# A matmul with LoRA, bound by DMA: fifteen partitions' second rows move from the software queue to a small store

## Chip, cores, metric

One core of a Trainium2 chip. The metric is the device time of one execution in microseconds (us); lower is better. The span in a profile is the time from the first to the last instruction and is about 1.3 us shorter than the time.

## The reference

```python
# x: 16 x 2048 x 256, W: 256 x 256, lora_A: 256 x 16, lora_B: 16 x 256, lora_E: 16; all float32
x_flat = x.reshape(-1, in_dim)                       # 32768 rows of 1024 bytes
y = x_flat @ W
lora_out = ((x_flat @ lora_A) * lora_E) @ lora_B
y = y + scale * lora_out
```

33.6 MB come in and 33.6 MB go out. The kernel folds the LoRA product into one 256 x 256 weight and then does one matmul, so bytes decide.

## The kernel before

The 32768 rows are four chunks of 128 partitions x 64 rows. A partition's 64 rows are one contiguous run of 64 KB in HBM. The ring in SBUF has three homes; a chunk is loaded, cast, turned, multiplied, and the result is written back to the home and stored from there. The order of loads (L) and stores (S) on the sync queue is a list:

```python
ORDER = [
    # ... cut: loads of chunks 0 to 3, stores of chunk 0
    ("S", 1, 0, 64),
    ("S", 2, 2, 62),      # chunk 2: rows 2 to 61 of each partition
    ("S", 3, 0, 64),
]
SHARED = 2
END_ROWS = 2
SHARES = (slice(108, 113), slice(0, 108), slice(113, P))
```

Chunk 2 is the shared one. Its rows 0, 1, 62 and 63 aren't in the large store; GpSimd's software queue writes them, in three shares of 5, 108 and 15 partitions:

```python
    def sync_program():
        # ... cut
            else:
                sync.wait_ge(s_done, -(-(c * ROWS + e) // CG) + NY)
                sync.dma_start(out=y_chunks[c, :, s:e, :], in_=at_home).then_inc(stored.get(op, stored_rest), 16)
        sync.wait_ge(shared_stored, 16 * len(SHARES))

    def share(engine, p, landed):
        def ends_of(at):
            return at[p].rearrange("p (q b) k -> p q b k", b=END_ROWS)[:, :: ROWS // END_ROWS - 1, :, :]

        engine.dma_start(out=ends_of(y_chunks[SHARED]), in_=ends_of(rows(SHARED, 0, ROWS))).then_inc(landed, 16)

    def gpsimd_program():
        # ... cut: the casts
        gpsimd.wait_ge(s_done, (SHARED + 1) * ROWS // CG + NY)
        for p in SHARES:
            share(gpsimd, p, shared_stored)
```

A large hardware store goes evenly to the 16 DMA engines, 8 partitions each. The software shares do not: they are there to give some engines less. The wait for the shares stands ahead of the closing barriers, the wait for the large stores behind them.

## Time and profile before

| | before |
|---|---|
| time, median of the first 3 runs / of 6 | 161.19 / 161.13 us |
| span of the profiled execution (its time: 161.41) | 160.1 us |
| bytes moved, mean rate | 67.41 MB, 421 GB/s |
| PE busy, ACT busy | 60%, 41% |
| last store issued, landed | 122.8, 160.0 us |

The DMA engines are busy from start to end, and compute is over at 122.7 us. The prediction below shows the lines.

In what follows, "large piece" is one hardware packet of 61440 or 65536 bytes (one partition of chunk 2 or 3), and "software packet" one packet of the shares (4096 bytes: one partition, two rows at either end). The trace has a start, a duration, a size and a queue for each packet and no engine number. The engines can be told apart nevertheless: on one engine a packet nearly always starts 3 to 4 ns before the end of the one before it, and each engine must have 8 pieces of each large store. I followed all 16 through the tail in this way; tables from it are in plain fences. A "heavy" engine is one of the twelve that carry ten software packets, a "light" one is one of the four that carry two.

### The profile page before, as it was taken

Reading aid. Unit: us, or ns where it says so; the run is one execution under the profiler, and the core shown is the slowest. Engines: PE = TensorE matmul, PEld = TensorE weight load, DVE = VectorE, ACT = ScalarE, POOL = GpSimd, SP = SyncE. Lnnn points to the kernel's source line nnn. Section 1 sums busy time; section 2 is a strip of 40 time slices with the busy share of each in tenths; the row PEclk is TensorE's granted clock in tenths of the full one; section 3 lists DMA queues with packets and bytes.
Section 4 is the critical chain, followed back from the end, with each engine's and each line's share of the span. In section 5 each row is a group of like instructions: output and inputs, shape, how many; then the busy total and the mean of one; then the engine's idle time right before and its main releaser. Section 6 shows DMA issues by size and latency. Waiting matters only on the chain.

```text
span 160.1 us, 2042 instructions
## 1 busy us (share of the span) xinstructions
PE 95.3 (60%) x782; PEld 83.3 (52%) x782; DVE 46.1 (29%) x67; ACT 66.3 (41%) x66; POOL 63.3 (40%) x41
## 2 busy tenths in 40 slices
PE   2749999999999910000799999999993000000000
PEld 1235899999999900000699999999992000000000
DVE  0113355555555510000155555555551000000000
ACT  3000577777777730000077777777775000000000
POOL 1044676777767100003676768686850000000000
PEclk9999999999999985555599999999999555555555
DMA  7999999999979997989999999996997998999965
GB/s 270 426 442 436 411 446 434 475 401 401 598 311 524 442 344 328 481 348 442 430 461 393 475 434 401 524 491 295 524 462 308 481 484 354 480 432 390 523 295 248
DMA packets 2449, 67.41 MB, mean 421 GB/s; under 512 B 512, under 2 KB 528, under 8 KB 784
## 3 DMA queue, kind: packets, MB, share of 16 engines
q1 hardware_dynamic: 2016, 66.60, 97.2%
q0 software_dynamic: 224, 0.52, 0.9%
q10 hardware_dynamic: 208, 0.28, 0.5%
q14 instruction: 1, 0.01, 0.0%
HBM read 33.85 MB, written 33.55 MB: 421 GB/s over the span
## 4 chain that ended last, share of the span: by engine, by line
PE 41%; DMA 32%; POOL 2%; ACT 1%; issue 0%; SPq 0%; ACTq 0%; POOLq 0%
DMA out_dram<-ring 27%; PE psum_y L271 26%; PE psum_xt L251 14%; DMA ring<-in_x_dram 5%; POOL stage L194 2%; PE psum_y L297 1%; ACT ring L217 1%; SPq L146 0%; ACTq L217 0%; POOLq L193 0%
## 5 line engine op out<-in xcount | busy, mean ns | idle before, releaser
L217 ACT COPY ring<-psum_y 128x1024 f32 x64 | 64.8, 1013 | 54.3 <-PE psum_y L271 54.3
L194 POOL CAST stage<-ring 128x2048 bf16<-128x2048 f32 x32 | 60.6, 1896 | 52.8 <-DMA out_dram<-ring 22.1
L271 PE MATMUL psum_y<-weff,xt 128*128 128x256 bf16 x512 | 68.5, 278 | 0.0
L240 DVE COPY xt<-psum_xt 128x1024 bf16<-128x1024 bf16 x64 | 44.3, 691 | 62.9 <-PE psum_xt L251 62.9
L251 PE MATMUL psum_xt<-ident,stage 128*128 128x128 f32 x260 | 41.3, 283 | 23.4 <-POOL stage L194 23.4
L271 PEld LDWEIGHTS psum_y<-weff,xt 128*128 128x128 bf16 x512 | 51.3, 100 | 6.0
L251 PEld LDWEIGHTS psum_xt<-ident,stage 128*128 128x128 f32 x260 | 31.6, 146 | 26.3 <-issue 25.2
L283 PE MATMUL psum_y<-ident 128*128 128x512 f32 x4 | 3.8, 1101 | 2.9 <-POOL ident L172 2.9
L283 PEld LDWEIGHTS psum_y<-ident 128*128 128x128 f32 x4 | 1.2, 324 | 3.9 <-POOL ident L172 2.9
L167 POOL DMA_DIRECT2D out_dram<-ring x3 | 2.0, 675 | 1.5 <-PE psum_y L271 1.5
L222 DVE TENSOR_SCALAR stage<-psum_y,e_sb 16x256 f32<-16x256 f32 x1 | 0.5, 472 | 7.2 <-PE psum_y L289 7.2
L211 ACT ACT_TABLE_LOAD x1 | 1.3, 1283 | 2.1 <-SPq L312 2.1
L297 PE MATMUL psum_y<-stage 16*128 16x256 f32 x4 | 2.1, 670 | 0.0
L231 DVE COPY xt<-psum_xt 128x1024 bf16<-128x1024 bf16 x1 | 0.7, 692 | 3.8 <-PE psum_xt L251 3.8
L297 PEld LDWEIGHTS psum_y<-stage 16*128 16x128 f32 x4 | 1.2, 319 | 0.5 <-issue 0.3
L234 DVE TENSOR_TENSOR weff<-stage,psum_y 128x512 bf16<-128x512 f32 x1 | 0.7, 686 | 1.4 <-PE psum_y L297 1.4
L289 PEld LDWEIGHTS psum_y<-ident,a_sb 128*16 128x16 f32 x2 | 0.3, 137 | 1.2 <-issue 1.2
L170 POOL MEMSET ident<- 128x128 f32 x1 | 0.2, 205 | 1.7 <-SPq L312 1.7
L289 PE MATMUL psum_y<-ident,a_sb 128*16 128x128 f32 x2 | 0.6, 421 | 0.0
L172 POOL TENSOR_SCALAR_AFFINE_SELECT ident<-ident 128x128 f32<-128x128 f32 x1 | 0.3, 283 | 0.2 <-POOL ident L170 0.2
L211 ACT COPY one<-ident 128x1 f32<-128x1 f32 x1 | 0.2, 191 | 0.0
L334 POOL MEMSET const-float32-0.0<- 128x1 f32 x1 | 0.1, 93 | 0.2 <-issue 0.2
(3 smaller groups left out, 0.3 us busy)
## 6 DMA issues: line engine op xcount, KB each, us to landing
ring<-in_x_dram SPq DMA_DIRECT2D x4, 4096.0 KB, 24.6
out_dram<-ring SPq DMA_DIRECT2D x1, 7680.0 KB, 37.1
ring<-in_x_dram SPq DMA_DIRECT2D x2, 3072.0 KB, 17.0
out_dram<-ring SPq DMA_DIRECT2D x1, 5120.0 KB, 43.0
out_dram<-ring SPq DMA_DIRECT2D x1, 3072.0 KB, 42.7
ring<-in_x_dram SPq DMA_DIRECT2D x1, 2048.0 KB, 7.9
out_dram<-ring POOLq DMA_DIRECT2D x1, 432.0 KB, 31.3
stage<-in_W_dram ACTq DMA_DIRECT2D x1, 256.0 KB, 2.8
```

What stands on the lines that cost most here:

```text
L167: engine.dma_start(out=ends_of(y_chunks[SHARED]), in_=ends_of(rows(SHARED, 0, ROWS))).then_inc(landed, 16)
L194: gpsimd.tensor_copy(out=stage[n % NS][:], in_=rows(c, b, b + CAST)).then_inc(s_stage[n % NS], 1)
L211: scalar.copy(out=one[:], in_=ident[:, :1])
L217: scalar.copy(out=to, in_=psum_y[i % NY][:]).then_inc(s_free[(i + NY) % UNROLL], 1)
L231: vector.tensor_copy(out=xt[0][:], in_=psum_xt[0][:].bitcast(BF16)).then_inc(s_xt[0], 1)
L234: vector.tensor_add(out=weff[:], in0=w_sb, in1=psum_y[1][:, :KT, :]).then_inc(s_free[0], 1)
L240: vector.tensor_copy(out=xt[g % NX][:], in_=psum_xt[g % NT][:].bitcast(BF16)).then_inc(s_xt[g % UNROLL], 1)
L251: ins = tensor.transpose(psum_xt[i % NT][:, b, :], words[:, at * CG + b, :], ident[:])
L271: ins = tensor.matmul(psum_y[i % NY][:, b, :], xt[i % NX][:, b, t::KT], weff[:, t, :], start=(t == 0), stop=(t == KT - 1),)
L283: ins = tensor.matmul(psum_y[1][:, :2, :], ident[:], ident[:, None, :].to_broadcast([P, 4, P]), start=True, stop=True)
L289: ins = tensor.transpose(psum_y[0][:R, t, :P], a_sb[:, t, :], ident[:])
L297: ins = tensor.matmul(psum_y[1][:, t, :], ate[:, t, :], b_sb, start=True, stop=True)
```

## The change

The last 15 partitions give the software queue only rows 0 and 63. Their rows 1 and 62 are written by a small store of 15 x 2 x 1024 bytes on the sync queue, between the large stores of chunks 2 and 3. By its form, the intent seems to be to take a little load from one DMA engine, since a store of 15 partitions uses 15 engines. Compute is unchanged.

```diff
-END_ROWS = 2
-SHARES = (slice(108, 113), slice(0, 108), slice(113, P))
+LAST = slice(113, P)
+SHARES = ((slice(108, 113), 2), (slice(0, 108), 2), (LAST, 1))
...
-    n_rest = sum(op[0] == "S" and op not in waited for op in ORDER)
+    n_rest = 1 + sum(op[0] == "S" and op not in waited for op in ORDER)
...
-                sync.wait_ge(s_done, -(-(c * ROWS + e) // CG) + NY)
+                sync.wait_ge(s_done, (c * ROWS + (ROWS if c == SHARED else e)) // CG + NY)
                 sync.dma_start(out=y_chunks[c, :, s:e, :], in_=at_home).then_inc(stored.get(op, stored_rest), 16)
+                if c == SHARED:
+                    second = slice(1, ROWS - 1, ROWS - 3)
+                    to, of = y_chunks[c, LAST, second, :], rows(c, 0, ROWS)[LAST, second, :]
+                    sync.dma_start(out=to, in_=of).then_inc(stored_rest, 16)
...
-        for p in SHARES:
-            share(gpsimd, p, shared_stored)
+        for p, n in SHARES:
+            share(gpsimd, p, n, shared_stored)      # n rows at either end
```

More of the change, by code (lines that the diff above doesn't have):

```diff
@@ L158, in sync_program, with share @@
             else:
-                sync.wait_ge(s_done, -(-(c * ROWS + e) // CG) + NY)
+                sync.wait_ge(s_done, (c * ROWS + (ROWS if c == SHARED else e)) // CG + NY)
                 sync.dma_start(out=y_chunks[c, :, s:e, :], in_=at_home).then_inc(stored.get(op, stored_rest), 16)
+                if c == SHARED:
+                    second = slice(1, ROWS - 1, ROWS - 3)
+                    to, of = y_chunks[c, LAST, second, :], rows(c, 0, ROWS)[LAST, second, :]
+                    sync.dma_start(out=to, in_=of).then_inc(stored_rest, 16)
         sync.wait_ge(shared_stored, 16 * len(SHARES))
-    def share(engine, p, landed):
+    def share(engine, p, n, landed):
         def ends_of(at):
-            return at[p].rearrange("p (q b) k -> p q b k", b=END_ROWS)[:, :: ROWS // END_ROWS - 1, :, :]
+            return at[p].rearrange("p (q b) k -> p q b k", b=n)[:, :: ROWS // n - 1, :, :]
         engine.dma_start(out=ends_of(y_chunks[SHARED]), in_=ends_of(rows(SHARED, 0, ROWS))).then_inc(landed, 16)
```

## The prediction

> **What bounds the kernel now.** I read the page of the profile first, then the chain of waits, the waits of the store queue, and the DMA view in narrow windows.
>
> ```profile
> PE   2749999999999910000799999999993000000000
> DMA  7999999999979997989999999996997998999965
> DMA packets 2449, 67.41 MB, mean 421 GB/s; under 512 B 512, under 2 KB 528, under 8 KB 784
> q1 hardware_dynamic: 2016, 66.60, 97.2%
> q0 software_dynamic: 224, 0.52, 0.9%
> HBM read 33.85 MB, written 33.55 MB: 421 GB/s over the span
> ```
>
> The matrix engine rests in about half of the slices; the DMA engines rest in none. 67.41 MB have to move whatever the order is, and the windows view gives 434 to 441 GB/s in the stretches without a gap (8 to 32 us, 74 to 150 us). 67.41 MB at 436 GB/s are 154.6 us of the 160.1 us span. What remains, 5.5 us, is the start, one lull near 58 us (loads to stores) and the tail. Compute is over long before the end: the answers of the timeline and of the store queue's waits are
>
> ```profile
> 121.70 1.01 ACT L217 COPY ring<-psum_y 128x1024 f32 x1 [0.30 <-PE psum_y L271]
> 122.83 0.33 SPq L160 DMA_DIRECT2D out_dram<-ring  x1
> ```
>
> ```profile
> SPq L160 <- PE psum_y L271: 54.6, 3, 27.1
> SPq L160 <- PEq L305: 19.4, 1, 19.4
> SPq L308 <- SPq L308: 3.8, 1, 3.8
> ```
>
> The last store is issued at 122.83 and lands 37.2 us later: the last 37 us are a queue being emptied. The last of the three lines says how far the two kinds of store differ at the end. The wait for the software queue's three shares ends near 155 us; after the closing barriers the core still sits 3.8 us in the wait for the big stores. So a share that lands up to 3.8 us later costs nothing.
>
> The end is therefore the last of 16 DMA engines, and the question is which one and why. The trace does not number them, but the DMA view in a narrow window counts a packet where it starts, so single engines can be seen. From 119.4 to 121.4 us (40 slices of 50 ns), where the first 61440-byte piece of chunk 2 starts on each engine, one piece is 1229 GB/s:
>
> ```profile
> DMA  0099999099099090000000000900000900000000
> GB/s 0 0 1229 1229 2458 2458 1229 0 1229 1229 0 3687 1229 0 1229 0 0 0 0 0 0 0 0 0 0 1229 0 0 0 0 0 1229 0 0 0 0 0 0 0 0
> ```
>
> 14 engines start it between 119.50 and 120.15, one at 120.65 and one at 120.95: two engines are late. From 156.1 to 160.1 us (slices of 100 ns), where each engine starts its last 65536-byte piece, one piece is 655 GB/s:
>
> ```profile
> DMA  9909999000090000000000000000300000000000
> GB/s 1311 1966 0 1311 2621 1311 655 0 0 0 0 655 0 0 0 0 0 0 0 0 0 0 0 0 0 0 0 0 82 0 0 0 0 0 0 0 0 0 0 0
> ```
>
> 14 starts lie before 156.8 and one at 157.2 (the sixteenth was before the window). A piece takes 2.42 us by its packet record, so the last engine ends at 159.70, and 0.37 us later the span ends. The next engine ends at 159.13. One engine is alone with the end by 0.57 us.
>
> Following the packets of each engine by their end and next start (a packet starts about 4 ns before the one ahead of it on the same engine ends) gives the software queue's part. 12 engines carry ten of the 4096-byte packets (two rows at either end of one partition), 4 engines carry two. That is 128 in all. The last engine is one of the twelve, with one packet of the 108-partition share's nine and one of the 15-partition share, and none of the 5-partition share; the other late engine (120.95) is one of the four light ones, and it catches up.
>
> **What the Trainium skill says.** "DMA: Bandwidth & Descriptors", section "Why a DMA increments its semaphore by 16 and not by 1": the number of engines k is the largest up to 16 that divides the slowest dimension, the hardware path takes the lowest-numbered k, and the software path takes k consecutive ones from a round-robin cursor. The trace agrees in kind: 5, then 108 as 12 times 9, then 15 from a moving cursor must give 11 engines with 9+1, one with 1+9 and four with 1+1, and that is what I count. With the cursor at c: the four light engines are c+1 to c+4, and the 15-wide share skips c. The same page, "Queues, rings and completion order", says an engine goes round its queue rows by packets. The trace shows it: a 4096-byte packet of 159 ns lies between two large ones. The page's "Latency and other measured facts" says engines 7 and 15 are usually slower; the records carry no engine number, so this trace can't say whether the late one is 15.
>
> **The change part by part.** No instruction of PE, DVE, ACT moves; the order of the programs is the same except for one more store on SP and a halved inner size of the last software store. The waits are equal too: for chunk 2, 192 rows over groups of 4 is 48, and the ceiling of 190 over 4 was 48.
>
> 1. The 15-partition share halves: on 15 engines (all but c) one 4096-byte packet of 159 ns becomes one of 2048 bytes. A 2048-byte packet of the weight load took 81 to 84 ns. Removed: 159 - 84 = 75 ns on each of the 15.
> 2. The small store brings the second rows back on the hardware queue, in 15 partitions, so k = 15: the lowest 15 engines, 0 to 14. Each gets two rows of 1024 bytes; a 1024-byte packet of the lora_B load took 46 ns, and a semaphore packet 9 ns. Added: 2 x 46 + 9 = 101 ns on each of engines 0 to 14, nothing on engine 15.
> 3. Sum per engine: +26 ns on 0 to 14; -75 ns on engine 15. If c is among 0 to 14, c gets +101 ns (it was skipped, and has 10 packets). If c is 15, engine 15 is unchanged. Total bytes stay.
> 4. The issue of the small store costs SP about 0.34 us (the median of the five stores' issues). It follows the issue of chunk 2's store, about 103 us (122.83 less the wait of 19.4 us above), and SP then waits those 19.4 us for the last chunk anyway. The last store's data starts on the engines near 138 us, 15 us after its issue, so no engine can run dry.
> 5. GpSimd's three issues take 2.02 us in all; the third writes the same number of descriptors, now shorter. Off the path: it lands 5 us before the end.
>
> So the only term on the path is that of the last engine: -75 ns if it is engine 15, +26 ns otherwise. It can't be c, which would have a packet of the first share. The bound of any gain from moving load is 0.57 us, the distance to the next engine, and the change moves far less. I think the edit is meant to spare engine 15, and give -75 ns a chance of 60%: 0.6 x -75 + 0.4 x 26 = -35 ns.
>
> **The rivals.** (a) The last engine is not number 15 and gets 26 ns more: 161.22. For: numbers are not in the records, and its lateness (0.5 us in the first chunk already) may come from the start. Against: the store would then have no purpose. (b) Small descriptors hurt more than their time: 1024-byte writes beside others, or the small store's packets waiting for write receipts before the big ones go on. That would be perhaps 0.1 to 0.3 us on 15 engines, and since they have 0.57 us until they are last, mostly hidden: up to 161.4. For it, some 4096-byte packets took 331 to 524 ns and not 159; against it, only four of 128 did, at one moment. (c) The four light engines lost about 0.2 us per large piece while the software queue ran; if that comes from its bytes or its duration, halving the last share relieves them. But they aren't the last, so the time stays. (d) The late engine loses up to 0.4 us in single packets (a 32768-byte store took 1.63 us in place of 1.21 near 99.7 us); if this falls elsewhere in another build, the time moves by 0.2 to 0.4 us either way, more than the change itself.
>
> **Range and chances.** 161.19 - 0.04 gives 161.15 us. The three runs of before lie within 0.17 us, and the terms above within 0.2 us; (b) and (d) set the width: 160.80 to 161.45. 2% would be 3.2 us, more than all that lies between the DMA's bare transfer and compute's hidden end can yield here; I keep 1% on either side for what I can't see.
>
> **What would show each step.** Right: the same 67.41 MB; under the software queue 113 packets of 4096 and 15 of 2048 bytes; 30 more rows of 1024 bytes on the hardware queue between chunks 2 and 3; one late engine in the same windows, its last piece starting within 0.1 us of 157.2. The step of engine 15 is right if the late engine has no small packets between 61440 and 65536 bytes. Wrong: the late engine has them, or another engine is last; gaps between the two big stores on the engines; the wait of 3.8 us gone, which would mean that the shares now end last.

## The result

161.64 us (median of 6, 161.28 to 161.97) against 161.13 us before (median of 6, 160.91 to 161.24): +0.5 us. The ratio is 1.0032, interval 1.0016 to 1.0048. A ratio here is the mean time of one kernel's fast runs over the mean of the other's fast runs of the same rounds, so it isn't quite the ratio of the medians. The change is slower, by little, but clear of the noise, and outside the predicted range (160.80 to 161.45).

The page of the changed kernel shows the parts that were predicted:

```profile
DMA packets 2494, 67.41 MB, mean 422 GB/s; under 512 B 527, under 2 KB 573, under 8 KB 829
q1 hardware_dynamic: 2061, 66.63, 97.5%
q0 software_dynamic: 224, 0.49, 0.8%
HBM read 33.85 MB, written 33.55 MB: 421 GB/s over the span
```

The bytes are equal. The hardware queue has 45 packets more: 30 rows of 1024 bytes at 46 ns and 15 semaphore writes. The software queue has as many packets and 30 KB less: 113 of 4096 bytes and 15 of 2048, the latter at 84 ns. The waits of the store queue are nearly the same too:

```profile
SPq L160 <- PEq L309: 18.4, 1, 18.4
SPq L312 <- SPq L312: 3.6, 1, 3.6
```

So the shares still end before the large stores (3.6 us in the last wait, 3.8 before), and SP's issue of the small store (0.98 us, not the 0.34 us that the prediction took) delays nothing: the wait behind it is 18.4 us in place of 19.4. One line of the DMA issues (size, us from issue to landing) differs more. First before, then the changed kernel:

```profile
out_dram<-ring POOLq DMA_DIRECT2D x1, 432.0 KB, 31.3
```

```profile
out_dram<-ring POOLq DMA_DIRECT2D x1, 432.0 KB, 25.4
```

The share of 108 partitions was not touched, and it lands 6 us sooner (25.7 us in the repeat below). Something let the software queue go faster. The DMA view from 138 to 142 us, where the engines go from chunk 2's store to chunk 3's, shows what. Before:

```profile
DMA packets 90, 2.11 MB, mean 527 GB/s; under 512 B 25, under 2 KB 25, under 8 KB 60
q1 hardware_dynamic: 45, 1.97, 115.0%
q0 software_dynamic: 45, 0.14, 8.8%
```

And the changed kernel:

```profile
DMA packets 174, 1.97 MB, mean 493 GB/s; under 512 B 60, under 2 KB 90, under 8 KB 148
q1 hardware_dynamic: 87, 1.73, 102.4%
q0 software_dynamic: 87, 0.24, 15.8%
```

87 software packets (semaphore writes counted) start in these 4 us and not 45. In these traces an engine takes its queues in turn, as the letters below show. Next to large pieces, the software queue gets one packet per 2.42 us. Next to packets of 46 ns and 9 ns it gets its turns at once: on each of the 15 engines two rows and one semaphore write are three extra turns, and a run of software packets goes through. Written as letters, one of the heavy engines reads (a, B: large pieces of chunks 2 and 3, S: software packet of 4096 bytes, s: of 2048 bytes, 1: small row, dot and comma: semaphore writes of the hardware and software queue, underscore: an 8-byte packet of the software queue in place of data):

```
before   aa_a,aSaSaSaSaS.SBSBSBSB,BSB,BB.
changed  aa_a,aSaSaSaSaS.S1S1S.SB,BsB,BBBBB.
```

This by itself costs no bytes. The profiled execution of the changed kernel (161.28 us) was the fastest of its six, and doesn't show the loss well: its last two engines end at 159.42 us (a light one) and 159.38 us. The next section has a slower one.

### The profile page after: what moved, and what is told of

Same layout as the page of the kernel before. It is cut to its first block, busy times and chain, and to the rows that moved or that the text cites. A ratio compares the mean times of both kernels' runs of the same rounds, so it can differ in the third digit from the quotient of the medians.

```text
span 159.9 us, 2043 instructions
## 1 busy us (share of the span) xinstructions
PE 96.4 (60%) x782; PEld 84.0 (53%) x782; DVE 46.1 (29%) x67; ACT 66.3 (41%) x66; POOL 63.2 (40%) x41
## 4 chain that ended last, share of the span: by engine, by line
PE 42%; DMA 32%; POOL 2%; ACT 1%; issue 0%; SPq 0%; ACTq 0%; POOLq 0%
DMA out_dram<-ring 27%; PE psum_y L275 26%; PE psum_xt L255 14%; DMA ring<-in_x_dram 5%; POOL stage L198 2%; PE psum_y L301 1%; ACT ring L221 1%; SPq L146 0%; ACTq L221 0%; POOLq L197 0%
## 5 line engine op out<-in xcount | busy, mean ns | idle before, releaser
L275 PE MATMUL psum_y<-weff,xt 128*128 128x256 bf16 x512 | 69.6, 281 | 0.0
```

Of the source, the lines that this page charges most:

```text
L275: ins = tensor.matmul(psum_y[i % NY][:, b, :], xt[i % NX][:, b, t::KT], weff[:, t, :], start=(t == 0), stop=(t == KT - 1),)
```

## The experiments

Fifteen runs in all.

**The same kernel again.**

> The changed kernel once more, unaltered, to see whether its +0.5 us (161.64 against 161.13) repeats and on which engine. All theories but chance: 161.5 to 161.8, 0.3 to 0.6 us above the kernel before of the same rounds. Theory chance (that chip or that hour): within 0.15 us of before. If it repeats, the trace should show one DMA engine whose last 65536-byte piece starts later than 157.0 us, or all engines later by 0.3 us.

161.66 us against 161.12: ratio 1.0024 (1.0010 to 1.0038), and its profiled execution took 161.66. It repeats. The starts of the last large piece on each engine, 156.1 to 160.1 us in slices of 100 ns (655 GB/s is one piece):

```profile
DMA  9909999900000090000000030000000000000000
GB/s 655 655 0 1966 1966 655 1311 655 0 0 0 0 0 0 655 0 0 0 0 0 0 0 0 82 0 0 0 0 0 0 0 0 0 0 0 0 0 0 0 0
```

One engine starts its last piece at 157.5, 0.6 us after all the others. Following it back, it isn't late when it begins chunk 2 (119.99, in the middle of the field). It loses the time in a run of software packets:

```
one engine, run of the changed kernel again      start us   took ns   usual ns
software packet, 4096 bytes                       139.067       273        159
software packet, 4096 bytes                       139.378       278        159
software packet, 4096 bytes                       139.695       353        159
software packet, 4096 bytes                       140.063       461        159
first large piece of chunk 3                      140.521      2418       2418
```

That is 729 ns of excess on one of 16 engines. The mean over all 16 of the time at which they end is unchanged: 158.88 us before, 158.90 here. The last ends at 159.93. The first profile of the changed kernel has the same in smaller measure: one engine with 499 ns (packets of 234, 481 and 261 ns, with others of 159 between), which ends at 159.38. There the light engine ends later still (159.42), so 499 ns did not set the end; 729 ns did, by 0.63 us over the next engine (159.30).

Slow software packets as such are not new. Summed over all 16 engines, the excess is 1.07 us in the trace of before and 1.09 and 0.97 us in the two of the changed kernel. In the trace of before the slow ones (331 to 524 ns, near 151 us, with no small rows about) lie on four engines, one each, and three of these are light. What differs is where they fall: several on one heavy engine.

**Without the small store** (wrong result: 30 rows are never written).

```diff
-                if c == SHARED:
-                    second = slice(1, ROWS - 1, ROWS - 3)
-                    ... sync.dma_start(out=to, in_=of).then_inc(stored_rest, 16)
```

> Wrong result on purpose: the small store is left out, its 30 rows are never written; the halved share stays. Theory S: within 0.15 us of the kernel before (30 KB less are 0.07 us less). Theory H: +0.3 to +0.6 us. The difference of this run to the changed kernel is what the small store costs: S 0.3 to 0.6 us, H under 0.1 us.

161.05 against 161.12, ratio 0.9994 (0.9980 to 1.0007). No cost of the halved share is seen; what is lost comes with the small store.

```profile
DMA  9090990900000000000000030000000000000000
GB/s 655 0 1311 0 2621 1966 0 1966 0 0 0 0 0 0 0 0 0 0 0 0 0 0 0 82 0 0 0 0 0 0 0 0 0 0 0 0 0 0 0 0
```

No engine is alone here: all last pieces that the window shows start before 156.9.

**The second rows as a fourth software share.**

```diff
-    (the small store)
+        gpsimd.dma_start(out=y_chunks[SHARED, LAST, second, :], in_=...).then_inc(shared_stored, 16)
```

> Undoes one part: the second rows of the last 15 partitions go as a fourth share on the software queue, no small store on the hardware queue. Theory S (the small hardware store costs the time): back to the kernel before, within 0.15 us. Theory H (the halved rows on the software queue, 1024-byte runs, cost it): as slow as the changed kernel, +0.3 to +0.6 us. Theory L (any change of the program shifts how late single engines are before 119 us): either, and the trace shows the lateness already at the first piece of chunk 2's store.

163.84 against 161.12, ratio 1.017. None of the three theories said that, and the reason is one that I should have reckoned with. Its waits of the store queue have no wait for the large stores left:

```profile
SPq L160 <- PEq L308: 19.4, 1, 19.4
SPq L351 <- PEq L351: 1.4, 2, 1.2
```

The wait of 3.6 us at the end is gone: a fourth share needs two more turns on each engine (data and semaphore write), and with large pieces a turn is 2.42 us. Its last semaphore write starts at 159.48 us, with the closing barriers still to come behind it. So this run says nothing on the small store; it shows what the slack of the shares is worth: 3.8 us are less than two turns (4.84).

**The small store behind the last large store.**

```diff
-                if c == SHARED:
+                if c == N_CHUNKS - 1:
```

> The small store is issued behind the last chunk's store and not between the two big ones. Theory S by its place (small rows between large pieces, and the turns of the software queue that they open, slow the last pieces): back to within 0.15 us of before, or up to 0.1 us above, since 92 ns of small rows now end the engines 0 to 14. Theory S by its mere presence, or H: +0.3 to +0.6 us as the changed kernel.

161.29 against 161.12, ratio 1.0007 (0.9993 to 1.0021). The same bytes, on the same engines, in another place: the loss is gone within the noise. The 92 ns of small rows at the very end would make up what is left, but that is not shown.

**The small store ahead of chunk 2's store.**

```diff
+                (the small store)
                 sync.dma_start(out=y_chunks[c, :, s:e, :], in_=at_home)...
-                (the small store)
```

> The small store is issued ahead of chunk 2's large store, so its rows run near 119.5 us, before the first software packet (123 us). Theory B (bunching: between two large stores the small packets give the software queue three more turns within 0.3 us on each of 15 engines, its packets then run nearly back to back, and on one engine several of them take 230 to 480 ns in place of 159, 0.5 to 0.9 us in sum): nothing to bunch, so within 0.15 us of the kernel before, and no software packet with more than 150 ns of excess near 139 us but for the share of the light engines. Theory P (the small store costs by its presence, wherever it is): +0.3 to +0.6 us.

161.09 against 161.08, ratio 1.0007 (0.9985 to 1.0030; one of its six runs was 161.97). The small rows run near 119.5 us, when the software queue has nothing yet. Theory P, the cost of mere presence, falls.

**The small store from ScalarE's queue.**

```diff
+        scalar.wait_ge(s_done, (SHARED + 1) * ROWS // CG + NY)      # after the copies
+        scalar.dma_start(out=to, in_=of).then_inc(stored_rest, 16)
```

> The changed kernel with the small store issued from ScalarE's queue once its copies are done (about 122.7 us): another ring, whose two rows take turns with chunk 2's large pieces. Theory B: no bunch, within 0.15 us of before. Theory P: +0.3 to +0.6 us. If the engine that the small store spares sets the end, it might be up to 0.1 us faster than before.

161.05 against 161.08, ratio 0.9996 (0.9981 to 1.0012). The small rows now take turns with large pieces. No loss, and no gain either: sparing one engine earns nothing.

**One row of all partitions between the large stores** (the shares of the kernel before, untouched).

```diff
-    sync.dma_start(out=y_chunks[c, :, s:e, :], ...)
+    m = 61 if c == SHARED else e
+    sync.dma_start(out=y_chunks[c, :, s:m, :], ...)
+    if c == SHARED:
+        sync.dma_start(out=y_chunks[c, :, m:e, :], ...)
```

> The kernel before with its shares as they were; only the last row of chunk 2's large store goes out as a store of its own behind it, 128 partitions of 1024 bytes, 8 small packets on each engine in the place where the small store is in the changed kernel. Theory B: more turns, the whole software queue runs off in one bunch: as slow as the changed kernel or slower, +0.4 to +1.5 us, with many slow software packets near 139 us on one engine. Theory E (it has to do with the share halved, with 15 partitions or the engine left out): within 0.2 us of before[...].

161.88 against 161.08, ratio 1.0045 (1.0029 to 1.0061). Neither the halved share, nor the 15 partitions, nor the spared engine is needed. With 8 small packets per engine the loss is at least as large as in the changed kernel (the intervals overlap). Its packet records have seven slow software packets, of 282 to 626 ns, within 1.5 us. The starts of the last large pieces:

```profile
DMA  0099999990000000900000000000000000000000
GB/s 0 0 1311 2621 655 1966 655 655 655 0 0 0 0 0 0 0 655 0 0 0 0 0 0 0 0 0 0 0 0 0 0 0 0 0 0 0 0 0 0 0
```

Again one engine is alone: it ends at 160.12, the next at 159.36. Followed back from its end, it has software packets of 360 and 494 ns just before chunk 3's store, 0.54 us of excess; what it carried before them could not be told apart from its neighbours' packets.

**The last 16 rows instead of one.**

```diff
-    m = 61 if c == SHARED else e
+    m = 46 if c == SHARED else e
```

> As the last, but the second store is the last 16 rows: 8 packets of 16384 bytes (611 ns) on each engine. The software queue has the same number of turns, but 0.6 us apart. Theory B by spacing: software packets keep apart, within 0.2 us of before. Theory B by early emptying (what matters is that the queue empties near 139 to 144 us, whatever the spacing): +0.4 us or more.

161.19 against 161.08, ratio 1.0004 (0.9989 to 1.0020). As many turns, 0.6 us apart, and no loss clear of the noise. The software packets are not all quick, though: seven of them took 259 to 714 ns, against what the theory said. But three of these seven lie on light engines, which have time to spare, and no heavy engine has more than 315 ns in sum.

**The last row behind the last large store** (control).

```diff
-    if c == SHARED: ... (second store)
+    if c == N_CHUNKS - 1: ... (second store)
```

> Control of the run with the last row as a store of its own (161.88 us against 161.08): the same store of 128 x 1024 bytes, issued behind the last chunk's store. Theory B: the software queue is empty by then or nearly, no bunch; 0 to 0.3 us above before, for 8 more descriptors per engine and small packets at the very end. Theory R (128 small writes cost in themselves): +0.6 us or more as in that run.

161.09 against 161.08, ratio 1.0003 (0.9985 to 1.0022). 128 small writes are not dear in themselves.

**A contiguous pair of rows instead of two single ones.** The small store takes rows 62 and 63, the software share rows 0 and 1 (so the share's two rows lie together too).

```diff
-                    second = slice(1, ROWS - 1, ROWS - 3)
+                    second = slice(ROWS - 2, ROWS)
```

> The changed kernel, but the small store takes the last two rows (one contiguous run of 2048 bytes per partition) and the software share the first two: the same bytes on the same engines, in the same place, with one small data packet per engine between the large stores instead of two, so two extra turns for the software queue (data, semaphore) instead of three. Theory B (bunching): fewer software packets back to back, +0.1 to +0.4 us over before. Theory P (any small store there): +0.4 to +0.6 us. Theory R (it is the two scattered 1024-byte writes, not the turns): within 0.1 us of before.

161.18 against 161.08, ratio 1.0006 (0.9991 to 1.0020). As many bytes in the same place, and the loss is gone within the noise. This left two readings: two extra turns and not three, or no packets of 1024 bytes.

**A gap between the large stores**. Chunk 3's store waits until chunk 2's has landed.

```diff
+                if c == N_CHUNKS - 1:
+                    sync.wait_ge(chunk_2_stored, 16)
```

> Built to look, not to be fast: the kernel before, whose last store is issued only once chunk 2's large store has landed, so for about 2 us the software queue has the engines to itself and no small hardware packet is there. Theory B in its strict form (software packets back to back slow one another on some engine): several packets of 4096 bytes above 230 ns, one engine with 0.3 to 0.9 us of excess near 138 to 140 us. If instead all 4096-byte packets of the twelve heavy engines take 159 ns in the bunch, the small hardware writes are needed as well. The time itself rises by 1.5 to 3 us.

162.62 us, one run. In the window from 138 to 142 us the software queue runs off in one bunch, before chunk 3's first piece starts at 140.70:

```profile
q0 software_dynamic: 125, 0.31, 19.3%
```

All its 4096-byte packets there took 159 ns, but one with 172. So the strict form of my theory falls: here software packets back to back did not slow one another.

**One small row instead of two** (wrong result: row 1 of 15 partitions is never written).

```diff
-                    second = slice(1, ROWS - 1, ROWS - 3)
+                    second = slice(ROWS - 2, ROWS - 1)
```

> Wrong result on purpose: the changed kernel with only row 62 of the last 15 partitions in the small store (row 1 is never written): one 1024-byte packet per engine, two extra turns as with the contiguous pair. Theory T: like the pair, within 0.2 us of before. Theory K: most of the changed kernel's +0.5 us, at least +0.25.

161.15 against 161.08, ratio 1.0005 (0.9992 to 1.0018), like the pair. Two extra turns, with 1024-byte packets: within the noise of before. In its trace one engine does lose 477 ns in software packets, but it ends at 159.42 us, and the engine behind it at 159.31. So two turns can bring a run of slow packets too; here it cost 0.1 us.

**The last two and the last four rows between the large stores.**

```diff
-    m = 61 if c == SHARED else e
+    m = 60 if c == SHARED else e      # and 58
```

> As the run with the last row as a store of its own between the large ones (161.88), but with the last two rows: 8 packets of 2048 bytes (84 ns) per engine, as many turns. Theory T (turns close together slow the software packets on one engine): +0.5 to +0.8 us. Theory K (packets of 1024 bytes are needed): within 0.2 us of before.

> The same with the last four rows: 8 packets of 4096 bytes (159 ns) per engine. Theory T by spacing: between the 1 row (+0.8) and the 16 rows (+0.1), +0.2 to +0.6 us. Theory K: within 0.2 us of before.

Two rows: 161.32 against 161.08, ratio 1.0021 (1.0006 to 1.0035). Four rows: 161.46, ratio 1.0026 (1.0013 to 1.0039). These stores have no packets of 1024 bytes, and with four rows the loss is clear, so theory K falls: the size isn't needed. Theory T had said +0.5 to +0.8 us for two rows; the medians give +0.24, so its size was missed. The dose runs, with 16 rows as the last point, against the length of the packets that part the turns:

| rows in the second store | its packets, per engine | ratio to before |
|---|---|---|
| 1 | 8 of 46 ns | 1.0045 |
| 2 | 8 of 84 ns | 1.0021 |
| 4 | 8 of 159 ns | 1.0026 |
| 16 | 8 of 611 ns | 1.0004 |

Two and four rows cannot be told apart. In the run with two rows the engine that ends last (159.63 us) has about 0.4 us of excess in software packets (262, 396 and 227 ns in the chain as it can best be followed).

**One row between the large stores, and a gap behind it**.

```diff
+                if c == N_CHUNKS - 1:
+                    sync.wait_ge(chunk_2_stored, 32)      # the large store and the row
```

> To look only: the run with the last row as a store of its own, and the last chunk's large store issued only when both have landed, so that small hardware packets and software packets alternate while no engine moves large pieces. If small hardware packets beside software packets are enough: software packets above 230 ns on one engine again, 0.3 us or more in sum. If large pieces on the other engines are needed too: all at 159 ns, as in the run with the gap alone.

163.57 us, one run. From 138 to 142 us:

```profile
q0 software_dynamic: 119, 0.30, 19.0%
```

Small rows and software packets alternate as in the run without the gap, and the 4096-byte software packets together took 9 ns longer than usual. The difference is that chunk 3's store is held back: the last pieces of chunk 2 end at 139.32, and the first of chunk 3 start at 141.64. It does not settle the matter, for in the run without the gap the first of the seven slow packets (285 ns, from 138.45) was over before any piece of chunk 3 had started (138.78).

**What is settled and what is not.** Settled is that the small store costs the time by its place: between the two large stores it costs, left out, ahead, behind or from another queue it does not. A loss clear of the noise came only with three or more extra turns whose packets take up to 159 ns; for two turns the intervals still allow up to 0.3 us. In the two kept traces of the slowest executions without a gap or a fourth share (the repeat, 161.66 us, and the single row between, 161.82 us), one heavy engine has a run of slow software packets and ends last, alone by 0.6 and 0.8 us. That chunk 3's large pieces must already move on other engines rests on the two looks with a gap, one execution each. The other timed executions have no kept trace, so the link from slow packets to the lost time is seen in these two executions and argued for the rest. Open is what the packets meet there, and why several of them fall on one engine. In one trace the slow engine is the one that the 15-partition share skips, in another it is not, so that doesn't decide it. Without engine numbers in the trace I can't say whether it is one physical engine.

## Why the prediction was wrong

- **What bounds the kernel** held in kind: the end is the last of 16 DMA engines, and compute, issues, waits and the landing of the shares played no part (3.6 us of slack in place of 3.8).
- **The sum per engine** held in its terms: 46, 84, 159 and 9 ns are all in the trace of the changed kernel.
- **The step that failed is the third part of the change**, "+26 ns on 0 to 14". It counted what the small packets take themselves. It left out what they do to the order: three extra turns for the software queue on each of 15 engines. What stood in its place is an excess of 499 and 729 ns on one heavy engine in the two traces of the changed kernel. The first did not set the end (a light engine did, at 159.42); the second did, and that execution took 161.66 us. I had quoted the rule of turns and applied it to the bytes only.
- **Rival (b)** named the right part, the small store beside the large ones, but a wrong cause (the small writes themselves: the runs ahead and behind speak against it) and a wrong cushion: "they have 0.57 us until they are last". That 0.57 us was the lateness of one engine in one execution, the profiled one, whose time of 161.41 us lay above every timed run. That engine began chunk 2's store at 120.69 us after it had lost 0.42 us in one packet near 99.7 us. In the other traces that I could follow no heavy engine starts later than 120.35, but for the run with the fourth software share (120.54). In the run without the small store the last two engines end at 159.30 and 159.26: the cushion was near zero for a heavy engine.
- **The step of engine 15** is, in its first half, as the Trainium skill says ("DMA: Bandwidth & Descriptors", "Why a DMA increments its semaphore by 16 and not by 1": the hardware path takes the lowest-numbered k engines, k being the largest number up to 16 that divides the slowest dimension, here 15). Exactly one engine has no small rows in the changed kernel's traces; that it is number 15 no trace shows. It ends at 159.19 and 159.12 us, ahead of the last by 0.2 to 0.8 us. In the traces that I followed without the loss the end belongs to a late light engine, whose 65536-byte pieces of chunk 1's store took about 2.58 us each and not 2.42, or to a heavy one within about 0.2 us of it. So the 75 ns that were saved lay beside the path, and the versions without the bunch (0.9994, 1.0007, 0.9996) gain nothing.
- **Rivals (a), (c) and (d)**: (a) is true of the end but is not the cause; (c) concerned the light engines: in the repeat three of them still lose 0.4 to 0.7 us in hardware packets and still end first, so it has no bearing; (d) was real, and it was in the very profile from which I took the cushion.
- **Two smaller slips**: the issue of the small store was taken as 0.34 us and took 0.98, off the path; and the late engine's "one packet of the 108-partition share's nine" should read all nine.

No version beat both kernels. The small store from ScalarE's queue and the one ahead of chunk 2 are equal to before, within the noise.

## What to carry to other kernels

A small transfer between two large ones changes whose turn it is: count the turns that it opens for the other queues, not only its bytes. Put such a transfer where the other queues are empty (ahead, here), or on a queue where it alternates with large packets. And where engines end within tenths of a microsecond of each other, take no slack from a single profile: compare its time with the timed runs first, and look at a second trace.

## What the Trainium skill lacked or had wrong

- "DMA: Bandwidth & Descriptors", "SWDGE vs HWDGE vs iDMA": it gives a packet, the unit of switching, as at most 4096 bytes preferably, in its account of the software path, and has no figure in bytes for the hardware path. The hardware queue here recorded a partition's run of 65536 bytes as one packet of 2.42 us, so beside it the software queue got one packet per 2.42 us.
- The same page, "Queues, rings and completion order": it has the round of turns, but not that a semaphore write is a turn of its own, as the letters show here (`B,B`: a large piece, a semaphore write of 9 ns, a large piece). A fourth share of 30 KB, two turns, made the kernel 2.7 us slower (163.84 against 161.12).
- No page has the loss found here: software packets that usually take 159 ns took 234 to 481 ns, several of them on one engine, when a small hardware store between two large ones let them bunch (+0.5 us); with the second large store held back, such a bunch ran at 159 ns, one packet at 172. Slow ones (331 to 524 ns) came without a small store too, one each on four engines, none of which ended last.
- The same page, "Why a DMA increments its semaphore by 16 and not by 1": it says that on this chip some software copies get 16 engines with rounded-up shares, and not which. Neither 108 nor 15 partitions did: 12 engines with 9 each, and 15 with one each, as its general rule has it.
